# A hybrid streaming encoder on one core: the recurrence of its RWKV-7 layer, by one pair of heads or by two in step

## The chip, the core and the metric

The kernel runs on one core of one Trainium2 chip. The metric is the device time of one execution in microseconds (us). A profile of one execution gives each engine's instructions: PE (matmuls; PEld are its weight loads), DVE, ACT, POOL, and SP, which here issues the DMAs. A trace row of the kernel always carries L210, the line of the helper that emits every instruction, so that rows are told apart by their tiles and shapes.

## The reference, cut to what matters

Four layers of width 2048 are run on 320 tokens (256 of a new stream, 64 of a running one): differential attention, sparse attention, RWKV-7, differential attention. Each is `x <- x + W_out (mixer(rmsnorm(x)) * silu(gate))`. The change is in the third, whose state update for each of 32 heads of 64 channels is

```
def step(st, inp):
    r_t, w_t, k_t, v_t, kk_t, a_t = inp
    sa = einsum('bhvk,bhk->bhv', st, -kk_t)
    st = st * w_t + sa[..., None] * (kk_t * a_t) + v_t[..., None] * k_t
    return st, einsum('bhvk,bhk->bhv', st, r_t)
...
o = (o - mean) * rsqrt(var + GN_EPS)      # per head
o = (o * ln_w + ln_b + bonus) * silu(g)
```

## The kernel before, in words

**Data.** Everything is kept channel-major: 16 tiles of 128 channels by 320 tokens. Index p (0 to 15) names such a tile, which in the RWKV-7 layer is a pair of heads. A projection is a set of output tiles; each is 16 x 3 products of a 128x128 weight block (split in a high and a low part in `ring`) with a 128x320 operand, in four pieces of four blocks. These are the wide products: psum<-op_b,ring for layers whose operand lies in op_b, psum<-op_a,ring for op_a.

**The recurrence** is computed in chunks of 64 tokens: four chunks of the new stream (c = 0 to 3) and one of the running stream. `chains()` (line 2201) goes over p. For each it runs `load_chain(p)` (1971), which waits for one of four sets of SBUF (SETS, 1953) and loads the record of p by DMA (rec_d, yr_d, two of v_d, the state). Then it spawns `chain(ps)` (2039), a task:
- `corners` (2007): per p a PSUM bank, ten 32x32 products, copies on ACT, ten more products, copies, and two scalings on POOL;
- four steps c, the first with the running stream's chunk beside it. A step is: products with 128 rows into a scratch, a copy on ACT, products with 64 rows, a copy with sign on ACT (`put`, 1990), products with 128 rows, the state update on DVE, and copies of the state to the two heads' places on ACT and DVE, from which the next step reads; POOL scales the state for it (`apart`, 2001);
- the set is handed back, and `gated(p)` (2114) is spawned: copy, mean, square, variance, a power on POOL, multiplication, ten 64x64 transposing products (psum<-cst or psum<-cst,arena), the gate; the PSUM bank is handed back behind that (2147).

In the loops of `corners` and `chain`, `for x in now` runs over all p of the task: each phase is emitted for all of them before the next phase.

**Beside it** PE works on the 16 g tiles of the gate's projection (768 wide products, op_b), and after them on the layer's output projection, whose first group is six output tiles together (`out_groups`, 709 and 763).

**What sets the order.** The program is laid down once, by a list scheduler at build time. The main loop (2352) lays down the wide products one block at a time; before each it calls `Sched.pump` (266), which lays down every task instruction whose inputs are ready by the scheduler's own reckoning (for PE with a slack of 400 ns). Where the main loop lacks something (an operand, weights, an accumulator) it calls `force` (288), which moves that reckoning on until a task gets further; nothing wide is laid down meanwhile. On the chip each engine and each DMA queue then runs its instructions in the order laid down.

**PSUM banks.** Of eight banks two are accumulators, and six (2 to 7) are shared (`Banks`, 347). Each p holds one from its corners to the end of `gated`. `start_group` (2335) takes a bank for every tile of a group before the group's first product, so that the group of six takes both accumulators and four of the six shared banks:

```
for mt in g.mts:
    acc = None if g.kis else banks.take_acc()
    while acc is None:
        if banks.free and (g.outer or len(banks.free) > 3):
            acc = banks.take1()
            break
        sched.force("accumulator")
```

In the trace a recurrence product (32, 64 or 128 rows, 32 or 64 columns) shows as two weight loads and two matmuls, a wide product as one.

Of the kernel before, what the change touches and what calls it, by code (L numbers as in the profile page):

```python
# [17 lines left out]
KT = 16  # L18
# [433 lines left out]
def hybrid_kernel(ctx: ExitStack, tc: tile.TileContext, a, o, layers=DEPTH):  # L452
# [62 lines left out]
    def spawn(stage, gen):  # L515
        assert stage.active or not stage.closed
        stage.active += 1
        sched.do(lambda: sched.tasks.append(Task(stage, wrap(stage, gen))))
# [1050 lines left out]
    def layer_c(li, opo, prev):  # L1569
# [388 lines left out]
        def prep_g():  # L1958
            for c in sets:
                G.memset(fields(c)[6], 0.0)  # L1960
            flags["prep_g"] = True
            yield

        def more_sets():

            while not sl.done():
                yield
            yield from wait(("inv", len(batches) - 1))
            sched.do(lambda: ES.free.extend(late))

        def load_chain(p):
            n = [i for i, ps in enumerate(batches) if p in ps][0]
            yield from wait(("inv", n), "prep_g")
            got = yield from SETS.get()
            cm, cs, y, kt, pc, zf, zb = fields(got.ap)
            Q.dma_start(got.ap[:, 0:REC], rec_d[p])
            Q.dma_start(c5(y, 160), y_rows(p))
            for e in range(2):
                Q.dma_start(cs[HALF[e], 320 - 320 * e:640 - 320 * e], v_d[p, HALF[e]])
                G.memset(cs[HALF[e], 320 * e:320 * e + 64], 0.0)  # L1980
            Q.dma_start(zf[:, 64:128], a["state_c_wkv"][p])
            flags["load", p] = got
# [213 lines left out]
        def start_g():  # L2196
            sk.closed = True
            spawn(sg, prep_g())
            spawn(sg, more_sets())

            def chains():
                for p in range(0, KT, 1):
                    ps = range(p, p + 1)
                    for x in ps:
                        yield from load_chain(x)
                    spawn(sg, chain(ps))
            spawn(sg, chains())
# [144 lines left out]
    for n, p in enumerate(pieces):  # L2352
# [17 lines left out]
        for i, b in [(i, b) for i in range(4) for b in range(len(woven))]:  # L2370
# [3 lines left out]
            ps = mt.acc.ap[0:m, 0:T]  # L2374
# [138 lines left out]
```

## Time and profile before

| | us |
|---|---|
| median of 3 runs | 2683.32 (2681.83 to 2683.38) |
| the profiled execution, its own time | 2683.37 |
| its span, first to last instruction | 2681.6 |
| PE busy in the span | 2627.8 (98%) |
| DVE, ACT, POOL busy | 1884.1, 1447.9, 421.4 |
| first product of the recurrence on PE | at 1700.90 |
| last product of the recurrence on PE | at 1903.06 |

Times in rows count from the start of the span. The stretch from 1700.90 to 1903.8 is the one in which the recurrence runs beside the g tiles. A window row gives the busy time of each engine and PE's granted clock (1.00 is full speed); a timeline row gives start, duration, engine, operation, tiles, shape, number of merged instructions and, in brackets, the engine's idle time ahead of it with what ended it.

### The profile page before, as it was taken

The page shows a single profiled execution, that of the slowest core. Times are in us where ns is not written, and L with a number is a line of the kernel's source. Part 1 is how long each engine was busy: PE and PEld are TensorE (multiplying, and loading weights), DVE is VectorE, ACT ScalarE, POOL GpSimd, SP SyncE. Part 2 cuts the span into 40 slices and gives each one's busy share as a digit, 9 for nine tenths or more (in the row PEclk, how much of TensorE's full clock was granted, in tenths as well). Part 3 has the DMA queues.
Part 4 walks back from the last instruction along what each step waited for, and adds up shares of the span by engine and source line. Part 5 has one row for each costly group of instructions (what it writes and reads, how often), then busy time and mean ns, then how long its engine had stood idle before and what let it go on. Part 6 is the DMA issues. An engine that isn't in the chain of part 4 may idle for free.

```text
span 2681.6 us, 53719 instructions
## 1 busy us (share of the span) xinstructions
PE 2627.8 (98%) x20012; PEld 2560.8 (95%) x20012; DVE 1884.1 (70%) x4035; ACT 1447.9 (54%) x3477; POOL 421.4 (16%) x787
## 2 busy tenths in 40 slices
PE   9999999999999999999999999999999999999997
PEld 9999999999999999999999988888999999999997
DVE  7777777665899766459876768457657777777654
ACT  5655555554444544535654544577545655555553
POOL 2000000001000000112011725587310000000011
PEclk9999999999999999999999999999999999999999
DMA  7544444455434334555667777766564444444353
GB/s 233 170 148 159 151 150 151 154 174 184 139 138 147 126 132 147 183 171 172 221 182 200 219 190 205 252 231 196 175 199 159 151 152 152 152 152 152 138 178 107
DMA packets 220876, 455.26 MB, mean 170 GB/s; under 512 B 83398, under 2 KB 149382, under 8 KB 186950
## 3 DMA queue, kind: packets, MB, share of 16 engines
q1 hardware_dynamic: 220614, 451.83, 51.0%
q8 instruction: 157, 2.57, 0.4%
q14 instruction: 105, 0.86, 0.1%
HBM read 394.20 MB, written 57.55 MB: 168 GB/s over the span
## 4 chain that ended last, share of the span: by engine, by line
PE 81%; DVE 6%; ACT 6%; DMA 4%; issue 2%; POOL 1%; SPq 1%; DVEq 0%; POOLq 0%; ACTq 0%
PE psum L210 81%; ACT arena L210 4%; DVE arena L210 4%; DVE ring L210 1%; DMA rec_d<-arena 1%; ACT ring L210 1%; SPq L210 1%; DMA raw<-in_a_w_in_dram 0%; DMA raw<-in_c_w_rkvg_dram 0%; POOL arena L210 0%; DMA arena<-yr_d 0%; DMA bv_d<-arena 0%; DVE op_b L210 0%; ACT op_b L210 0%; DMA yr_d<-arena 0%
## 5 line engine op out<-in xcount | busy, mean ns | idle before, releaser
L210 PE MATMUL psum<-op_a,ring 128*128 128x320 f32 x8496 | 1316.6, 312 | 8.8 <-ACT op_a L210 3.8
L210 PEld LDWEIGHTS psum<-op_a,ring 128*128 128x128 f32 x8496 | 1257.4, 189 | 14.9 <-ACT op_a L210 4.4
L210 ACT CAST ring<-raw 128x512 fp32r<-128x512 f32 (+2 forms) x1228 | 750.0, 618 | 772.7 <-PE psum L210 716.4
L210 DVE TENSOR_TENSOR ring<-raw,ring 128x512 fp32r<-128x512 f32 (+2 forms) x1228 | 855.1, 703 | 402.6 <-ACT ring L210 387.9
L210 PE MATMUL psum<-op_b,ring 128*128 128x320 f32 (+1 forms) x6240 | 990.0, 314 | 0.4 <-DVE arena L210 0.4
L210 PEld LDWEIGHTS psum<-op_b,ring 128*128 128x128 f32 (+1 forms) x6240 | 923.9, 188 | 10.9 <-DVE arena L210 0.7
L210 DVE TENSOR_TENSOR arena<-psum,arena 32x320 f32<-32x320 f32 (+1 forms) x535 | 260.6, 487 | 71.4 <-PE psum L210 61.7
L210 PE MATMUL psum<-arena 128*64 128x64 f32 (+7 forms) x3556 | 267.9, 248 | 8.8 <-DMA arena<-yr_d 3.3
L210 PEld LDWEIGHTS psum<-arena 128*64 128x64 f32 (+5 forms) x3556 | 224.9, 153 | 42.4 <-issue 13.0
L210 ACT ACTIVATE arena<-psum,smt 64x128 f32<-64x128 f32 (+5 forms) x384 | 157.8, 412 | 70.7 <-PE psum L210 49.7
L210 ACT COPY arena<-psum 128x384 f32<-128x384 f32 (+7 forms) x348 | 137.3, 401 | 102.4 <-PE psum L210 97.4
L210 POOL TENSOR_TENSOR arena<-arena 128x64 f32<-128x64 f32 (+25 forms) x282 | 175.7, 631 | 69.0 <-DVE arena L210 40.8
L210 POOL TENSOR_TENSOR smt<-smt,mhalf 128x3 f32<-128x3 f32 (+2 forms) x64 | 68.8, 1075 | 496.6 <-DVE smt L210 496.2
L210 PE MATMUL psum<-cst,arena 128*128 128x128 f32 (+3 forms) x899 | 124.9, 269 | 15.2 <-DVE arena L210 6.8
L210 PEld LDWEIGHTS psum<-cst,arena 128*128 128x128 f32 (+3 forms) x899 | 97.1, 138 | 27.5 <-DVE arena L210 10.1
L210 POOL MEMSET smt<- 128x3 f32 x64 | 6.4, 99 | 680.6 <-DVE smt L210 680.5
L210 POOL TENSOR_TENSOR ssum<-ssum,arena 128x320 f32<-128x320 f32 x70 | 65.3, 933 | 282.2 <-ACT arena L210 281.5
L210 ACT ACTIVATE arena<-arena 128x320 f32<-128x320 f32 (+1 forms) x208 | 90.4, 442 | 34.9 <-DVE arena L210 23.5
L210 ACT CAST op_b<-arena 128x320 fp32r<-128x320 f32 (+4 forms) x198 | 79.4, 417 | 52.4 <-DVE arena L210 32.8
L210 DVE TENSOR_TENSOR op_b<-arena,op_b 128x320 fp32r<-128x320 f32 (+4 forms) x198 | 87.7, 460 | 7.2 <-ACT op_b L210 7.1
L210 DVE TENSOR_TENSOR arena<-arena 64x320 f32<-64x320 f32 (+5 forms) x196 | 85.7, 449 | 2.1 <-ACT arena L210 0.3
L210 ACT CAST op_a<-arena 128x320 fp32r<-128x320 f32 (+2 forms) x127 | 55.8, 441 | 58.0 <-DVE arena L210 39.2
(115 smaller groups left out, 1330.7 us busy)
## 6 DMA issues: line engine op xcount, KB each, us to landing
raw<-in_a_w_in_dram SPq DMA_DIRECT2D x120, 1024.0 KB, 4.9
raw<-in_c_w_rkvg_dram SPq DMA_DIRECT2D x52, 1024.0 KB, 5.3
raw<-in_w_out_dram SPq DMA_DIRECT2D x46, 1024.0 KB, 5.2
raw<-in_b_w_in_dram SPq DMA_DIRECT2D x45, 1024.0 KB, 4.8
raw<-in_w_out_dram SPq DMA_DIRECT2D x72, 256.0 KB, 3.7
arena<-rec_d SPq DMA_DIRECT2D x16, 962.5 KB, 7.7
raw<-in_c_w_rkvg_dram SPq DMA_DIRECT2D x48, 256.0 KB, 3.9
out_dram<-arena SPq DMA_DIRECT2D x72, 160.0 KB, 4.6
```

Source lines behind the costliest of these rows:

```text
L210: return getattr(self.engines[op.eng], op.name)(*op.args, **op.kw)
```

## The change

`chains()` goes over p in steps of two and gives both to one `chain` task. Both loads stand ahead of that task. With four sets, two such tasks of two can be under way; before, four tasks of one.

```
             def chains():
-                for p in range(0, KT, 1):
-                    ps = range(p, p + 1)
+                for p in range(0, KT, 2):
+                    ps = range(p, p + 2)
                     for x in ps:
                         yield from load_chain(x)
                     spawn(sg, chain(ps))
```

No instruction is added or removed; the build lays them down in another order from the recurrence's first products on. In the rows below, 128x320 is a wide product, arena 32x32 a corner, arena 64x64 a product of a step (of 64 or 128 rows), cst 64x64 and cst,arena 64x64 a transposing product of `gated`.

On PE, where the recurrence begins (p = 0 and 1, beside the first g tiles), one piece of the difference:

```order
-L210 MATMUL psum<-op_b,ring 128x320 x9
-L210 MATMUL psum<-arena 32x32 x10
-L210 MATMUL psum<-op_b,ring 128x320 x12
-L210 MATMUL psum<-arena 64x64 x4
+L210 MATMUL psum<-op_b,ring 128x320 x30
+L210 MATMUL psum<-arena 32x32 x10
+L210 MATMUL psum<-op_b,ring 128x320 x3
+L210 MATMUL psum<-arena 32x32 x10
```

Products of the recurrence now come in blocks of two head pairs with fewer returns to the wide ones. From the first corner product to the last wide product of the output projection, the wide products stood in 106 blocks and now stand in 83; the recurrence's products, counted by their number of rows (32, 64 or 128), stood in 184 uniform blocks and now in 126.

On PE, where the g tiles end and the output projection (op_a) begins, before:

```order
L210 MATMUL psum<-cst,arena 64x64 x10
L210 MATMUL psum<-arena 64x64 x6
L210 MATMUL psum<-op_b,ring 128x320 x15
L210 MATMUL psum<-arena 64x64 x2
L210 MATMUL psum<-op_b,ring 128x320 x6
L210 MATMUL psum<-arena 64x64 x8
L210 MATMUL psum<-cst,arena 64x64 x10
L210 MATMUL psum<-op_a,ring 128x320 x45
L210 MATMUL psum<-cst 64x64 x10
L210 MATMUL psum<-op_a,ring 128x320 x723
```

and with the change, directly behind the last block of g products (three of them):

```order
L210 MATMUL psum<-arena 64x64 x56
L210 MATMUL psum<-cst 64x64 x10
L210 MATMUL psum<-cst,arena 64x64 x20
L210 MATMUL psum<-arena 32x32 x30
L210 MATMUL psum<-cst 64x64 x10
L210 MATMUL psum<-arena 32x32 x10
L210 MATMUL psum<-arena 64x64 x96
L210 MATMUL psum<-cst,arena 64x64 x10
L210 MATMUL psum<-arena 32x32 x10
L210 MATMUL psum<-cst,arena 64x64 x10
L210 MATMUL psum<-arena 32x32 x20
L210 MATMUL psum<-op_a,ring 128x320 x6
```

Before, only the last products of p = 15 stood behind the g tiles. Now 282 products of the recurrence stand in a row there: the second half of the last step of p = 8 and 9, the last two steps of 10 and 11, the whole of 12 and 13, and most of the corners of 14 and 15, whose steps stand among the first 162 wide products of the output projection.

On DVE in the same place, the mean of p = 10 (second row), its variance (fifth) and its multiplication (last), with the change:

```order
L210 SCALAR_TENSOR_TENSOR rstd<-psum,cvec,rstd 128x320
L210 SCALAR_TENSOR_TENSOR arena<-smt,arena 128x320
L210 SCALAR_TENSOR_TENSOR rstd<-rstd,cvec,cst 128x320
L210 SCALAR_TENSOR_TENSOR arena<-psum,cvec,arena 128x320
L210 TENSOR_REDUCE smt<-psum 128x5
L210 SCALAR_TENSOR_TENSOR arena<-arena,cvec 128x320
L210 TENSOR_TENSOR op_a<-rstd,op_a 128x320
L210 TENSOR_SCALAR smt<-smt 128x5
L210 TENSOR_TENSOR op_a<-arena,op_a 128x320
L210 TENSOR_REDUCE smt<-cst 128x5
L210 SCALAR_TENSOR_TENSOR cst<-smt,cst 128x320
L210 TENSOR_TENSOR arena<-arena,smt 128x320
```

The rows between belong to `gated` of p = 8 and 9 (the gate, rows with cvec and op_a) and of p = 11 (rows with cst), which end one group and lie on one engine together.

## Rows read from the trace of the kernel before

**Rows 1.** The page: busy time of PE, and its granted clock in 40 slices.
```profile
PE 2627.8 (98%) x20012; PEld 2560.8 (95%) x20012; DVE 1884.1 (70%) x4035; ACT 1447.9 (54%) x3477; POOL 421.4 (16%) x787
...
PEclk9999999999999999999999999999999999999999
```

**Rows 2.** Waits of PEld, 1700.5 to 1904: us in total, times, longest.
```profile
PEld psum L210 <- issue: 10.6, 54, 0.3
PEld psum L210 <- ACT arena L210: 10.6, 44, 0.8
```

**Rows 3.** Timeline of PEld in the recurrence.
```profile
1708.98 0.44 PEld L210 LDWEIGHTS psum<-op_b,ring 128*128 128x128 f32 x3
1709.61 0.31 PEld L210 LDWEIGHTS psum<-arena 64*64 64x64 f32 x8 [0.19 <-issue]
1709.99 0.45 PEld L210 LDWEIGHTS psum<-op_b,ring 128*128 128x128 f32 x3
...
1829.63 0.19 PEld L210 LDWEIGHTS psum<-arena 64*64 64x64 f32 x4 [0.19 <-ACT arena L210]
1829.89 0.45 PEld L210 LDWEIGHTS psum<-op_b,ring 128*128 128x128 f32 x3
...
1896.27 6.60 PEld L210 LDWEIGHTS psum<-op_a,ring 128*128 128x128 f32 x45
```

**Rows 4.** Timeline, ACT and DVE, one step of p = 15.
```profile
1891.38 0.28 DVE L210 SCALAR_TENSOR_TENSOR arena<-psum,arena 128x64 f32<-128x64 f32 x1
...
1891.69 0.24 ACT L210 COPY arena<-arena 64x64 f32<-64x64 f32 x1 [1.15 <-DVE arena L210]
...
1893.16 0.21 ACT L210 COPY arena<-psum 128x64 f32<-128x64 f32 x1 [0.34 <-PE psum L210]
```

**Rows 5.** Timeline of p = 15: corners, last step, last products, its multiplication in `gated`.
```profile
1867.13 0.39 PEld L210 LDWEIGHTS psum<-arena 32*32 32x32 f32 x20 [0.19 <-issue]
...
1892.75 0.20 PEld L210 LDWEIGHTS psum<-arena 128*64 128x64 f32 x4 [0.19 <-issue]
...
1895.04 0.43 PEld L210 LDWEIGHTS psum<-arena 128*64 128x64 f32 x12 [0.76 <-ACT arena L210]
...
1901.71 0.49 DVE L210 TENSOR_TENSOR cst<-cst,smt 128x320 f32<-128x320 f32 x1 [0.42 <-POOL smt L210]
```

**Rows 6.** Groups by form, 1690 to 1900: count | busy us, mean ns | idle ahead.
```profile
L210 ACT ACTIVATE arena<-psum 64x64 f32<-64x64 f32 x160 | 34.8, 217 | 12.6 <-PE psum L210 10.4
...
L210 ACT COPY arena<-arena 64x64 f32<-64x64 f32 x80 | 19.5, 243 | 13.7 <-DVE arena L210 11.5 <-DMA arena<-in_state_c_wkv_dram 1.1
L210 POOL TENSOR_TENSOR smt<-smt,mhalf 128x5 f32<-128x5 f32 x15 | 18.5, 1236 | 3.3 <-DVE smt L210 3.0
...
L210 ACT COPY arena<-psum 128x64 f32<-128x64 f32 x64 | 13.3, 213 | 11.1 <-PE psum L210 9.9
...
L210 ACT ACTIVATE arena<-psum 32x160 f32<-32x160 f32 x32 | 9.4, 293 | 1.0 <-PE psum L210 0.6
...
L210 DVE TENSOR_REDUCE smt<-psum 128x5 f32<-128x320 f32 x16 | 7.7, 482 | 4.1 <-ACT psum L210 4.1
...
L210 ACT ACTIVATE arena<-psum 128x320 f32<-128x320 f32 x14 | 6.1, 436 | 2.7 <-POOL arena L210 1.6 <-PE psum L210 0.8
```

**Rows 7.** Windows: length, busy time (count) of PE, PEld, DVE, ACT, POOL, PEclk, DMA.
```profile
1699.60:1706.30 6.70, 5.39 (x54) 4.94 (x55) 1.18 (x2) 2.85 (x9) 4.31 (x10) 0.50 1.09 331
1706.40:1895.00 188.60, 186.09 (x2928) 153.90 (x2927) 121.83 (x298) 136.05 (x503) 143.15 (x300) 1.00 0.64 207
```

**Rows 8.** Timeline of PEld where the recurrence begins.
```profile
1700.90 0.61 PEld L210 LDWEIGHTS psum<-arena 32*32 32x32 f32 x20 [3.56 <-DMA arena<-yr_d]
1701.58 2.37 PEld L210 LDWEIGHTS psum<-op_b,ring 128*128 128x128 f32 x9
```

**Rows 9.** Timeline of SP: the record of p = 15 is asked for.
```profile
1858.26 0.37 SPq L210 DMA_DIRECT2D arena<-rec_d  x1
```

**Rows 10.** The page's DMA issues: out<-in, count, KB each, us to landing.
```profile
arena<-rec_d SPq DMA_DIRECT2D x16, 962.5 KB, 7.7
```

## The prediction

> **What bounds the kernel now.** I read the page first: PE is busy for 98% of the span and its clock is full in every slice [rows 1]. So only two things can change the time: what PE spends on its own products, and stretches in which PE has nothing to do. Then the waits of the weight loads while the recurrence runs [rows 2]: 98 waits of 0.19 to 0.8 us, about 21 us together. Most of them are no wait for data: the timeline shows the same 0.19 wherever a block of wide products ends and a product of the recurrence begins [rows 3]. That is the first thing to see: today's recurrence is hidden almost completely, and what it costs beside its products is the change of kind. The second is how long the recurrence takes by itself: p = 15 goes from its corners at 1867.13 to its last products at 1895.04, 27.9 us for 20 corner products and 48 others [rows 5]. It is latency; it is hidden as long as wide products lie between its steps.
>
> **The change, term by term.** Nothing is added, so the sum is made of order alone.
>
> *Changes of kind, a gain.* In a run of 45 wide products one weight load follows another after (6.60 - 0.19) / 44 = 0.146 us. A block of three starts at 1708.98 and the next kind at 1709.61: 0.63, of which 3 x 0.146 = 0.44 is work, so 0.19 to 0.20 is the change. Eight loads of a recurrence product need 0.38 (1709.61 to 1709.99), four need 0.26 (1829.63 to 1829.89): 0.03 a load, and 0.14 for the change [rows 3]. The new order has 83 blocks of wide products for 106, and 126 uniform blocks of the recurrence for 184. 23 x 0.20 + 58 x 0.14 = 12.7 us saved.
>
> *A bare stretch, a loss.* The order has 282 recurrence products in a row behind the last g product. A group of two hands its two sets back together, so the next group's loads start late, and in the end the 768 g products are used up while four head pairs are still to come. The output projection cannot fill in: its first group needs four of the six shared banks, and two groups hold four until `gated` is through. Only behind p = 13's transposing products does a wide product come. Now each link has its full length. A step alone, from rows 4 to 6: product to ACT 1893.16 - 1892.75 = 0.41, copy 0.21, ACT to PE about 0.05, second product to ACT 0.41, two copies with sign 2 x 0.217, 0.05, third product to DVE 0.41, state update 0.28, DVE to ACT 0.03, copy 0.24, 0.05: 2.6 us [rows 4, 5, 6]. The second head pair of the group runs inside these gaps; I take 2.65 for both. The stretch is then:
> - the last two steps of p = 10 and 11, 5.3, with 8's and 9's last half step and `gated` on the same in-order ACT and DVE (some seven passes of about 0.44, 3.1; the group at 436 ns is the row for such a pass [rows 6]): 8.5;
> - `gated` of p = 10, whose bank p = 13 needs: from the last products at 1895.04 to the end of the multiplication at 1902.20 it took 7.2 [rows 5]; now six closing rows of 8 and 9 stand between its own on DVE, so I take no less: 7.2;
> - corners and first step of p = 12 and 13. ACT carries eight copies of 0.29, four of the state at 0.24, then two of 0.21, four at 0.22, eight more at 0.22, two of 0.24: 6.8, and three links of 0.41 [rows 4, 6]: 8.0;
> - three more steps: 8.0;
> - `gated` of 12 and 13: 7.2, and one POOL power of 1.24 more for the second [rows 5, 6]: 8.4.
>
> That is 40.1 us; I take 40. PE's own work in it is 212 x 2 x 0.03 + 70 x 2 x 0.016 (0.39 for 20 loads [rows 5]) + 23 x 0.14 = 18, done before as well. So PE waits 22 us. Bounds: with `gated` at the length of its parts (power 1.24, two sums at 0.48, five passes of about 0.45: 4.5 [rows 6]) and without the 3.1 of the others, 32; with 27.9 + 7.2 for p = 12 and 13 as p = 15 took it, and the first two items, 51 [rows 5]. The wait is 14 to 33. The value lies nearer the low end because p = 15's 27.9 has wide products in it that are gone here.
>
> *The clock.* Before the first corners PE waited 3.56 us [rows 8], and the granted clock then was 0.50 for 6.7 us [rows 7]: nine wide products took 2.37, (2.37 - 0.19) / 8 = 0.27 each for 0.146. The bare stretch has several waits of that size, so the clock should stand at its lower level, 1.2 GHz, where the projection begins: 6.7 us at 0.27 are 25 products, 3 us lost. Bounds 0 (the clock holds) and 6 (it is also low inside the stretch, where each of some 25 links with products grows by about 0.1). I take 3.
> The Trainium skill ("TensorE: Matmul & The Clock Gate", on the clock gate) says that an idle PE falls back to half its rate until it has been busy again. By that rule the term is at its upper end, 6; the trace agrees as far as the one episode in rows 7 goes.
>
> *Loads.* The loads of both stand ahead of a group's task, in the same SP queue as the weights, with the state's load behind the store of the old state. Before, p = 15's record was asked for at 1858.26 and its corners ran at 1867.13, 8.9 us later, with no wait [rows 5, 9]; the order keeps wide products for about such a time, but now two records come at once, for p = 4 to 11 twice. The price of a missed one is the first one's, 3.56 [rows 8]; between 0 and 4 x 3.56 I take 1.5, since none of the reloads was missed before.
>
> *After it* the steps of p = 14 and 15 have 162 wide products between them, three and more at each link, and `gated` behind them 45, as p = 15 had; I cost them at nothing. From the end of the output projection on PE's order is the same, so the rest shifts as a whole.
>
> Sum: -12.7 + 22 + 3 + 1.5 = +13.8 us on the profiled execution's 2683.37 (the median is 2683.32, no different): **2697**.
>
> **The rivals.**
> 1. *The stretch is shorter than thought and the saved changes win* (faster). For it: the 12.7 is the firmest term, from rows that repeat to 0.01 us, while the 40 is put together by hand. It decides where the bare stretch is under 18 + 12.7 = 30.7 us with the clock at full speed: at 25 us, 2683.4 - 12.7 + 7 = 2677.7, and 2670.7 if it costs nothing. Against it: 30.7 is under the low bound of 32.
> The Trainium skill ("TensorEngine Tiling (Array Packing)", Key Properties) says that changing the tiling mode drains TensorE; by this rule alone the change gains its 12.7 us and nothing more. The 0.14 and 0.20 of rows 3 agree with it.
> 2. *They cancel* (no change): a stretch of 28 to 35 us, the low bound with little loss of clock: 2681 to 2688.
> 3. *The reloads are late* (slower still): four times 3.56 in the middle of the stage, on top of the sum instead of 1.5: 2697 + 12.7 = 2710. For it: two records of 962.5 KB [rows 10] and their companions are asked for at once. Against it: no such wait before.
>
> **How the numbers follow.** About 0.2%, 5.4 us, is what a measurement of this kernel can tell from no change. I give the forecast 0.62, rival 1 0.10, rival 2 0.16, rival 3 0.12. Slower by more than that: 0.62 + 0.12 = 0.74; within it 0.16; faster 0.10. With the bounds of the wait alone the forecast runs from 2689 to 2708. The range reaches down over rival 2 and up over rival 3 with some of its spread: 2681 to 2713.
>
> **What would show it.** Right: wide products until about 1855, then some 40 us with PE's loads busy for less than half, the first op_a product at about 1894, the last transposing product at about 1934 (before, 1903, with 117 fewer wide products done); waits of PEld for ACT and DVE arena tiles of several us; a stretch at 0.50 in the granted clock there; ahead of it, the waits of 0.19 fewer by about a fifth or more. Wrong: a stretch under 31 us; the loss spread over the stage with DMA as releaser (rival 3); or a loss outside 1700 to 1935, for which this argument has no place.

## The result and the profile after

The changed kernel takes 2707.42 us (median of 4 runs, 2705.45 to 2709.12) where the kernel before took 2682.57 beside it: a ratio of 1.0088, 95% interval 1.0076 to 1.0100, 24.9 us slower. The forecast was 2697 in a range of 2681 to 2713. The profiled execution took 2709.12 us; its span is 2707.3.

The page of the changed kernel, busy time and granted clock, to be read against [rows 1]:

```profile
PE 2637.2 (97%) x20012; PEld 2571.9 (95%) x20012; DVE 1885.9 (70%) x4035; ACT 1453.7 (54%) x3477; POOL 425.1 (16%) x787
...
PEclk9999999999999999999999999997899999999999
```

The same number of products keeps PE busy 9.4 us longer, and two slices have lost clock, where before none had. Windows of the changed kernel tell where; the columns are those of [rows 7]:

```profile
1703.50:1857.20 153.70, 151.49 (x2217) 131.86 (x2217) 90.81 (x208) 105.48 (x372) 113.62 (x229) 0.98 0.66 213
1857.20:1908.00 50.80, 34.08 (x565) 28.20 (x564) 27.32 (x72) 24.70 (x93) 25.94 (x56) 0.59 0.47 148
1908.00:1946.60 38.60, 38.60 (x420) 34.30 (x414) 18.99 (x45) 20.25 (x65) 13.30 (x28) 0.92 0.30 95
```

The second window is the bare stretch: 282 recurrence products (564 loads), 28.2 us of loads in 50.8. Its ends and its inside in the timeline of PEld:

```profile
1856.62 0.45 PEld L210 LDWEIGHTS psum<-op_b,ring 128*128 128x128 f32 x3
1857.25 0.69 PEld L210 LDWEIGHTS psum<-arena 64*64 64x64 f32 x16 [0.19 <-ACT arena L210]
...
1865.09 1.36 PEld L210 LDWEIGHTS psum<-arena 128*64 128x64 f32 x24 [0.42 <-ACT arena L210]
...
1873.68 1.18 PEld L210 LDWEIGHTS psum<-cst,arena 64*64 64x64 f32 x20 [4.90 <-ACT psum L210]
...
1887.48 0.54 PEld L210 LDWEIGHTS psum<-arena 128*64 128x64 f32 x8 [1.18 <-ACT arena L210]
...
1891.05 0.30 PEld L210 LDWEIGHTS psum<-arena 128*64 128x64 f32 x4 [0.31 <-ACT arena L210]
...
1903.81 1.17 PEld L210 LDWEIGHTS psum<-cst,arena 64*64 64x64 f32 x20 [5.44 <-issue]
...
1908.06 1.57 PEld L210 LDWEIGHTS psum<-op_a,ring 128*128 128x128 f32 x6
1909.95 0.61 PEld L210 LDWEIGHTS psum<-arena 32*32 32x32 f32 x20 [0.33 <-issue]
1910.63 2.37 PEld L210 LDWEIGHTS psum<-op_a,ring 128*128 128x128 f32 x9
...
1945.91 0.66 PEld L210 LDWEIGHTS psum<-cst,arena 64*64 64x64 f32 x20 [0.19 <-issue]
```

The last g products start at 1856.62, the first op_a at 1908.06, the last transposing products at 1945.91. The first rows of the waits of PEld from 1700.5 to 1942 (us in total, times, longest), against [rows 2]:

```profile
PEld psum L210 <- ACT arena L210: 18.3, 59, 1.5
PEld psum L210 <- issue: 13.1, 40, 5.4
PEld psum L210 <- ACT psum L210: 4.9, 1, 4.9
PEld psum L210 <- DMA arena<-yr_d: 3.7, 1, 3.7
```

The one wait for a load is that of the very first corners, as before [rows 8]: no reload is late. Ahead of the stage, where the order of PE is the same in both kernels, the profiled execution had lost 2.6 us already (first corners at 1703.49, 1700.90 before [rows 8]); from the end of the stage on the two traces run parallel, 25.7 us apart. So some 23 of the 25.8 us between the two profiled executions arise between 1703 and 1946.

### The profile page after: what moved, and what is told of

The parts are those of the page before. It is cut to its first block, busy times and chain, and to the rows that moved or that the text cites. A ratio compares the mean times of both kernels' runs of the same rounds, so it can differ in the third digit from the quotient of the medians.

```text
span 2707.3 us, 53766 instructions
## 1 busy us (share of the span) xinstructions
PE 2637.2 (97%) x20012; PEld 2571.9 (95%) x20012; DVE 1885.9 (70%) x4035; ACT 1453.7 (54%) x3477; POOL 425.1 (16%) x787
## 4 chain that ended last, share of the span: by engine, by line
PE 79%; ACT 7%; DVE 6%; DMA 4%; issue 2%; POOL 1%; SPq 0%; DVEq 0%; POOLq 0%; ACTq 0%
PE psum L210 79%; ACT arena L210 6%; DVE arena L210 4%; DVE ring L210 1%; ACT ring L210 1%; DMA arena<-yr_d 1%; POOL arena L210 1%; DMA arena<-l_d 1%; DVE smt L210 1%; DMA raw<-in_a_w_in_dram 0%; DMA bv_d<-arena 0%; SPq L210 0%; ACT op_a L210 0%; DMA yr_d<-arena 0%; DMA arena<-in_x_dram 0%
## 5 line engine op out<-in xcount | busy, mean ns | idle before, releaser
L210 PEld LDWEIGHTS psum<-arena 128*64 128x64 f32 (+5 forms) x3556 | 229.7, 160 | 47.6 <-ACT arena L210 18.5
L210 ACT COPY arena<-psum 128x320 f32<-128x320 f32 (+8 forms) x350 | 137.1, 403 | 105.2 <-PE psum L210 99.3
L210 POOL TENSOR_TENSOR arena<-arena 128x64 f32<-128x64 f32 (+24 forms) x282 | 177.3, 633 | 74.1 <-DVE arena L210 45.1
L210 ACT CAST op_b<-arena 128x320 fp32r<-128x320 f32 (+4 forms) x198 | 79.7, 418 | 50.8 <-DVE arena L210 32.1
```

The lines of the kernel that those rows point to most:

```text
L210: return getattr(self.engines[op.eng], op.name)(*op.args, **op.kw)
```

## The experiments

There were twelve runs of ten new kernels, one of them twice, and of the changed kernel once more; the kernel before ran beside each. Their traces reach the first corner at different times (1699.6 to 1708.2), though the order of PE ahead of it is the same, so that stages are compared by their length. "Bare" products are recurrence products without a wide one between them, in the order laid down.

### A smaller first group, and its control

The first group of the output projection takes four tiles, so that it needs two shared banks and not four; the control does the same to the kernel before.

```
-        return ([Group(mts[0:(6 if li == 2 else 4)], ...
+        return ([Group(mts[0:(4 if li == 2 else 4)], ...
```

> The changed kernel, with one edit: the output projection's first group in this layer takes four output tiles instead of six, so two shared banks instead of four, and it can begin while two groups of head pairs still hold theirs. In the order laid down the first output-projection product now follows the g tiles at once; the longest runs of recurrence products without a wide one are 92, 70 and 38 instead of 282. Theory A (the bare stretch behind the g tiles is the loss: 50.8 us for about 18 us of PE's own work, and it exists because of the banks): about 33 us come back, and some 3 us of half clock behind it, so 2671; with up to 9 us of waits left in the three shorter runs, 2671 to 2680, below the kernel before by 3 to 12 us, which is the saving of changes of kind (91 wide blocks for 106, 126 uniform ones for 184). Rival B (pairs in step lose time all over the stage, by later loads or longer links, and the stretch is only where it becomes visible): the time stays over 2690. Rival C (the stretch is the loss, but the changes of kind are hidden anyway): 2682 to 2686, no faster than before.

> Control for the run with a first group of four: the kernel before with the same edit. Its group of six never waited for banks, so all theories expect the time of before within 3 us, 2680 to 2686. If it were faster by itself by 5 us or more, the group size would be a gain of its own and the other run would have to be read against this one.

The control: 2685.39 us, ratio 0.9997 (0.9988 to 1.0006). The changed kernel with it: 2701.43 us against 2685.28, ratio 1.0046 (1.0032 to 1.0060). Less than half of the loss has gone: theory A's size is wrong, and by the total alone rival B (over 2690) stands; the next section decides against it. The five times spread over 12.8 us (2692.59 to 2705.43) and the trace is that of the slowest. Its windows and timeline of PEld:

```profile
1860.80:1888.60 27.80, 27.78 (x406) 23.98 (x404) 19.64 (x47) 18.93 (x65) 15.54 (x34) 1.00 0.82 266
1888.60:1937.30 48.70, 37.11 (x604) 30.43 (x600) 27.71 (x71) 25.77 (x100) 24.80 (x52) 0.83 0.32 106
```

```profile
1914.51 1.39 PEld L210 LDWEIGHTS psum<-arena 128*64 128x64 f32 x40 [0.19 <-issue]
...
1929.57 0.19 PEld L210 LDWEIGHTS psum<-op_a,ring 128*128 128x128 f32 x1 [2.04 <-ACT op_a L210]
1930.80 1.12 PEld L210 LDWEIGHTS psum<-op_a,ring 128*128 128x128 f32 x5 [1.04 <-DVE op_a L210]
```

Where 50.8 us were bare, PE is now full for 28 us, and then it starves all the same. By 1914.51 it has done 144 op_a products, which is three quarters of the 4 x 48 of the group; by the order of the group the next ones need op_a of p = 12; they come at 1929.57, and they wait for op_a, from ACT and then from DVE. The banks were the gate that I had seen; behind it stands a second one, the operands, and a smaller group reaches it sooner.

### Cover that is not missing

If the rest of the argument holds, the change must pay where wide work is plentiful. Both kernels got 300 more wide products at the start of that group, with the scheduler's tasks between them:

```
             mt.acc = acc
+            if mt is g.mts[0] and len(g.mts) == 6 and not g.weave:
+                for i in range(3 * 100):
+                    if i % 3 == 0:
+                        sched.pump()
+                    model.emit(Op("PE", "matmul", (acc.ap[:, 0:T],), dict(lhsT=blk, rhs=op_b[:, 0, 0, :], ...
```

> The kernel before with 300 wide products more between the g tiles and the output projection (into an accumulator that is then overwritten; results unused), so that the recurrence has cover beyond its end. All theories: 2683 plus 300 x 0.146 = 43.8 us, 2725 to 2730; 108 wide blocks and 184 uniform ones in the order laid down. It is the control for the next run.

> The changed kernel with the same 300 wide products. No bare stretch is left in the order laid down (longest run without a wide product 42); 99 wide blocks for 108 of the control, 129 uniform ones for 184. Theory A (changes of kind cost 0.20 and 0.14 us, and all the rest of the loss is the missing cover): 9 x 0.20 + 55 x 0.14 = 9.5 us below the control, 2716 to 2720, clock 1.00. Rival N (the changes of kind cost nothing, or pairs in step bring new waits for loads, ACT or DVE even under cover): the control's time or more, 2725 to 2735.

Without the change 2725.45 us (2723.68 to 2728.62), with it 2719.19 (2717.29 to 2720.89): 6.3 us faster, two thirds of the 9.5; no time of one lies among the other's. Waits of PEld from 1699 to 1932, the kernel before first:

```profile
PEld psum L210 <- issue: 10.8, 56, 0.3
PEld psum L210 <- ACT arena L210: 9.8, 43, 0.6
```

```profile
PEld psum L210 <- ACT arena L210: 10.0, 43, 0.7
PEld psum L210 <- issue: 9.4, 49, 0.2
PEld psum L210 <- DMA arena<-yr_d: 4.7, 3, 3.7
```

Pairs in step bring almost no new wait while they are covered: 4.7 us for loads where the kernel before has 3.6. So the saving is real, and the loss of the change is missing cover; rivals B and N fall.

### PE kept busy in the bare stretch

```
                 sched.force("accumulator")
+                while g.outer and sched.tasks and model.clk["PE"] + 600.0 < sched.now:
+                    model.emit(Op("PE", "matmul", (g.mts[0].acc.ap[:, 0:T],),
+                                  dict(lhsT=blk, rhs=op_b[:, 0, 0, :], start=True, stop=True)))
```

> The changed kernel, with PE kept busy in the bare stretch: where the first group of the output projection lacks a bank and PE would run dry, a wide product into an accumulator that is already taken is added (98 of them, whose results are overwritten and used by nothing). They add 98 x 0.146 = 14.3 us of PE work into a stretch in which PE waits for 33. Theory A1 (ten of the eleven us by which the stretch is longer than my 40 come from PE running it at half clock): granted clock 1.00 throughout, stretch of 40 to 43 us, total 2693 to 2699. Rival L (the stretch is long because the links on ACT, DVE and POOL are long, whatever PE's clock): clock 1.00, but the stretch stays at 48 to 52 us, total 2703 to 2710. If the added products come in the way of the links, longer still.

> The kernel with 98 wide products added in the bare stretch once more, on another day's chip, because its first times spread over 10 us. From the first corner product to the layer's end its trace took 8 us less than the changed kernel's. If that is PE's clock, it comes again: granted clock 1.00, the stretch 44 to 46 us instead of 50 to 51, and a ratio to the kernel before of 1.004 to 1.007 where the changed kernel has 1.0076 and 1.0088. If the stretch is back at 50, it was chance.

> The changed kernel itself once more, on the chip of the three runs beside it, so that they can be read against it: 2705 to 2711, with the bare stretch of 49 to 52 us at half clock from 1857 on.

With the added products: 2705.39 us against 2685.28, ratio 1.0070 (1.0057 to 1.0083), and again, on another chip, 2699.83 against 2683.26, ratio 1.0063 (1.0050 to 1.0076). The changed kernel once more: 2708.03 against 2687.10, ratio 1.0076 (1.0061 to 1.0090). The mean of the ratios, 1.0067 for 1.0082, is 4 us in favour of the added work; the intervals overlap, so that the total alone says little, and the first total lies in rival L's range, not in A1's. The traces say more. From the first corner to the end of the span they take 996.1 and 997.2 us with the added products, 1003.8 and 1005.1 in the changed kernel. The stretch with the added products, twice, and in the repeated changed kernel:

```profile
1857.50:1903.00 45.50, 38.51 (x665) 32.47 (x663) 26.09 (x72) 23.78 (x93) 26.04 (x56) 1.00 0.53 165
```

```profile
1853.00:1900.80 47.80, 39.87 (x665) 33.80 (x663) 26.09 (x72) 23.90 (x94) 26.08 (x56) 0.96 0.51 157
```

```profile
1862.40:1912.70 50.30, 33.38 (x566) 27.50 (x564) 27.55 (x72) 24.67 (x94) 25.62 (x56) 0.62 0.49 149
```

The stretch is 2.5 to 5.3 us shorter, though 14 us of work are added. The clock is full in the first and nearly so in the second, where one block of nine wide products took 2.37 us for 1.32. Neither theory has it right: A1 said 40 to 43 us, L 48 to 52, and the repeat missed its 44 to 46. One step of p = 12 and 13, first with the added products (PEld, then DVE), then in the changed kernel (DVE; its PEld row of 1891.05 stands above):

```profile
1888.35 0.31 PEld L210 LDWEIGHTS psum<-arena 128*64 128x64 f32 x8 [0.19 <-issue]
...
1890.94 1.32 PEld L210 LDWEIGHTS psum<-op_b,blk 128*128 128x128 f32 x9
1892.46 0.31 PEld L210 LDWEIGHTS psum<-arena 128*64 128x64 f32 x8 [0.19 <-issue]
```

```profile
1890.68 0.28 DVE L210 SCALAR_TENSOR_TENSOR arena<-psum,arena 128x64 f32<-128x64 f32 x1 [2.95 <-PE psum L210]
```

```profile
1890.44 0.28 DVE L210 SCALAR_TENSOR_TENSOR arena<-psum,arena 128x64 f32<-128x64 f32 x1 [2.88 <-PE psum L210]
...
1894.25 0.28 DVE L210 SCALAR_TENSOR_TENSOR arena<-psum,arena 128x64 f32<-128x64 f32 x1 [2.66 <-PE psum L210]
...
1898.09 0.28 DVE L210 SCALAR_TENSOR_TENSOR arena<-psum,arena 128x64 f32<-128x64 f32 x1 [2.69 <-PE psum L210]
```

From the first product of the step to the state update it takes 1890.68 - 1888.35 = 2.33 us at full clock, and 1894.25 - 1891.05 = 3.20 at half. The half clock costs 0.87 us a step. The state copies follow within another 0.6, so a step at full clock would be 2.9 us long by the first head pair (an estimate; by the second, whose copies end 0.5 later, 3.4), where the changed kernel has 1894.25 - 1890.44 = 3.81. The added work itself takes some of the gain back: nine products, 1.32 us together, lie between the steps and make each one 1892.46 - 1888.35 = 4.11 long.

### What makes the g tiles run out early

> The changed kernel with half of the change undone: both loads still stand ahead of a pair of head pairs, but each head pair is a task of its own again, not in step. The order laid down is nearly that of before (115 wide blocks, 201 uniform ones; longest bare run 48). Theory A (what uses up the g tiles early is that two head pairs in step hand their sets and banks back together): no bare stretch; 2683 plus 9 x 0.20 + 17 x 0.14 = 4.2 us for more changes of kind, 2684 to 2690. Rival J (the joint load, which starts the second head pair's record late or early, is what costs): 2697 or more, with waits for loads or a bare stretch.

```
-                    spawn(sg, chain(ps))
+                    for x in ps:
+                        spawn(sg, chain([x]))
```

> The changed kernel with each head pair a task of its own, not in step, but the two sets of a group still loaded together and handed back together, when both head pairs are through. The prediction said that the joint hand-back is why the next loads start late and the g tiles run out (theory H). Theory E: it is the emission in step, in which each head pair's link waits for the other's copies on ACT, that makes a set's turn longer (64 us for the first turn where single head pairs took 47). H: the turn of the sets stays near 60 us and the time at 2700 or more. E: turns of 47 to 53 us, and 2683 plus 13 x 0.20 + 12 x 0.14 = 4.3 us for more changes of kind, 2684 to 2691, with no bare stretch (119 wide blocks, longest bare run 50).

```
-                got.rel()
+                flags["fin", p] = True
...
+        def back(ps):
+            yield from wait(*[("fin", p) for p in ps])
+            for p in ps:
+                flags["load", p].rel()
...
+                    spawn(sg, back(ps))
```

(The chains are single, as in the run before.) Loaded together but not in step: 2687.73 us, ratio 1.0011 (1.0002 to 1.0019). Handed back together as well: 2689.26 against 2686.61, ratio 1.0014 (1.0005 to 1.0023). Theory H falls, and so does rival J. The pace is read from SP's timeline, the loads of p = 0, 4 and 12: that of p = 4 waits for a set to come round once, that of p = 12 three times. Before:

```profile
1690.27 0.32 SPq L210 DMA_DIRECT2D arena<-rec_d  x1
...
1737.19 0.37 SPq L210 DMA_DIRECT2D arena<-rec_d  x1
...
1833.04 0.39 SPq L210 DMA_DIRECT2D arena<-rec_d  x1
```

The changed kernel:

```profile
1692.74 0.32 SPq L210 DMA_DIRECT2D arena<-rec_d  x1
...
1756.71 0.38 SPq L210 DMA_DIRECT2D arena<-rec_d  x1
...
1859.69 0.37 SPq L210 DMA_DIRECT2D arena<-rec_d  x1
```

Joint hand-back without step:

```profile
1691.28 0.32 SPq L210 DMA_DIRECT2D arena<-rec_d  x1
...
1742.74 0.37 SPq L210 DMA_DIRECT2D arena<-rec_d  x1
...
1842.64 1.37 SPq L210 DMA_DIRECT2D arena<-rec_d  x1
```

The first turn of a set takes 46.9 us before, 64.0 with the change, 51.5 with the joint hand-back alone; three turns take 142.8, 167.0 and 151.4. Loaded together alone, the same loads stand 46.1 and 143.9 us apart. So a third of the 24 us that the recurrence falls behind is the joint load and hand-back, nearly all of it the hand-back, and two thirds are the step itself. One piece of it shows in the first group, in the changed kernel's PEld and DVE and in the DVE of before:

```profile
1703.49 0.61 PEld L210 LDWEIGHTS psum<-arena 32*32 32x32 f32 x20 [3.71 <-DMA arena<-yr_d]
...
1710.93 0.39 PEld L210 LDWEIGHTS psum<-arena 32*32 32x32 f32 x20 [0.19 <-issue]
```

```profile
1723.00 0.28 DVE L210 TENSOR_SCALAR arena<-psum,arena 128x64 f32<-128x64 f32 x1 [4.46 <-ACT arena L210]
```

```profile
1712.61 0.28 DVE L210 TENSOR_SCALAR arena<-psum,arena 128x64 f32<-128x64 f32 x1 [3.41 <-PE psum L210]
```

p = 0 has its corners begun at 1703.49, but in step it stands until p = 1 has begun its own at 1710.93: its first state update comes 19.5 us after its first corner, before 11.7. PE is busy all the while with g products: nothing is lost there, it is only taken from the end.

### The pace alone, and half the pairs

> The kernel before with three sets of SBUF for single head pairs instead of four; no head pairs in step anywhere. Theory P (the loss comes from the pace of the recurrence: a set came round every 47 to 49 us before, every 64, 54 and 49 us with the change, so the g tiles run out too early, and the rest of the recurrence is bare): three places at 47 us give the same kind of loss without any pairing. In the order laid down 322 recurrence products stand bare behind the g tiles; at the change's excess of (50.8 - 18) / 282 = 0.116 us each that is 37 us, plus 3 of clock and 2.4 of more changes of kind (200 uniform blocks for 184): 2727, between 2712 and 2740. Rival S (what costs is the emission in step itself: both head pairs on the in-order ACT and DVE, double bursts): less than 2700, since nothing is in step.

```
-        sets = [lg.ap(SET) for _ in range(4)]
+        sets = [lg.ap(SET) for _ in range(3)]
```

> The changed kernel with single head pairs for p = 0 to 7 and pairs in step for p = 8 to 15. In the order laid down 216 recurrence products stand bare. Theory P: 216 x 0.116 = 25 us, plus 3 of clock, less 5.5 for 12 and 22 fewer changes of kind: 2707, between 2698 and 2714. Rival S (cost in proportion to the pairs in step): half of the loss of 25: 2695 to 2698. The two lie close, the next run parts them.

```
-                for p in range(0, KT, 2):
-                    ps = range(p, p + 2)
+                for p in [*range(0, 8), *range(8, KT, 2)]:
+                    ps = range(p, p + (1 if p < 8 else 2))
```

> The reverse: pairs in step for p = 0 to 7, single head pairs for p = 8 to 15. In the order laid down 350 recurrence products stand bare, although nothing is in step in that stretch. Theory P: 350 x 0.116 = 41 us, plus 3 of clock, less 11.2 for 31 and 36 fewer changes of kind: 2718, between 2706 and 2726, slower than with all pairs in step. Rival S: half of the loss, 2695 to 2698.

```
+                for p in [*range(0, 8, 2), *range(8, KT)]:
+                    ps = range(p, p + (2 if p < 8 else 1))
```

All beside 2687.10 us of the kernel before. Three sets: 2711.24, ratio 1.0089 (1.0075 to 1.0103). Single first, pairs last: 2702.24, ratio 1.0057 (1.0045 to 1.0070). Pairs first, single last: 2693.81, ratio 1.0027 (1.0017 to 1.0037). Rival S falls with the first, where nothing is in step and the loss is the change's own. Theory P has the size in the second alone; where single head pairs stand bare it is 16 and 24 us too high, outside its range both times, and in the last run S's figure is the nearer, though the measured time is below S's range too. The windows of the bare stretch, of the three runs in this order:

```profile
1871.40:1918.20 46.80, 37.17 (x646) 30.71 (x645) 24.64 (x67) 28.64 (x114) 25.65 (x63) 0.62 0.41 126
```

```profile
1875.40:1910.20 34.80, 23.62 (x433) 20.44 (x432) 17.23 (x50) 18.42 (x75) 19.22 (x41) 0.67 0.31 90
```

```profile
1865.70:1910.30 44.60, 35.49 (x702) 29.76 (x700) 26.37 (x74) 29.09 (x120) 29.72 (x67) 0.73 0.55 164
```

A bare product costs 50.8 / 282 = 0.180 us and 34.8 / 216 = 0.161 where two head pairs in step stand there, 46.8 / 322 = 0.145 and 44.6 / 350 = 0.127 where single chains do; PE is busy for 37.2 and 35.5 us there instead of 34.1. That single chains fill each other's gaps is the likely reason; no run tests it. The clock is higher in the last alone (0.73; the change has 0.59 and 0.62). With the prediction's 18 / 282 = 0.064 of PE's own work for each product, and its prices for the changes of kind, the sum can be made for all four:

| kernel | bare stretch | own work | changes of kind | sum | measured |
|---|---|---|---|---|---|
| the change | 50.8 | 18.0 | -12.7 | +20.1 | +24.9, +20.9 |
| three sets | 46.8 | 20.6 | +2.4 | +28.6 | +24.1 |
| single, then pairs | 34.8 | 13.8 | -5.5 | +15.5 | +15.1 |
| pairs, then single | 44.6 | 22.4 | -11.2 | +11.0 | +6.7 |

Made afterwards, with the measured stretch, the sum is within 5 us each time. No kernel that was run beats the kernel before.

## Why the prediction was right, and where it was off

**What bounds the kernel:** right. PE is full until 1857, nothing outside the stage has moved for a reason that the change gives, and the changed sum is made of order alone.

**Changes of kind, -12.7:** the sign is right, the size somewhat high. With full cover 6.3 us came back of 9.5 worked out by the same prices. The waits fell as said, from 43 + 37 to 31 + 34 before 1857, about a fifth; but that sign proves little, because by then PE had done 1680 loads other than those of the g tiles, where it had done 1958 before, a seventh fewer. For each load the waits are 5% fewer.

**The bare stretch, 40 us:** this term is the mis-sized one. Its place and its start are right (wide products until 1857, said 1855), and so are the banks, as the first of two gates: the smaller group showed the operands behind them. But it lasts 50.8 us, to 1908 and not to 1894. Item by item, from the timeline above: 7.8 for 8.5, 8.6 for 7.2, 13.8 for 8.0 (corners and first step), 10.9 for 8.0 (three steps, to the end of p = 12's last state update at 1898.4), 9.7 for 8.4. More than half of the 10.8 us too many lies in the corners and first step, 2.9 in the three steps. The step of 2.65 us was a little short at full clock (2.9 to 3.4, as worked out above); at half clock it is 3.8, and some 42 of the 50.8 us ran so. What of the corners' 5.8 is the clock alone, no run separates. Two of the signs named beforehand did not come: PE's loads were busy for 28.2 of 50.8 us, more than half, and the waits for ACT arena tiles were 1.5 us at most (the two long waits, 4.9 and 5.4, have other releasers).

**The clock, 3 us with an upper end of 6:** this is where it failed. I let the clock fall in the waits and cost it behind the stretch. Windows inside the changed kernel's stretch, PEclk being the third number from the end:

```profile
1857.20:1862.60 5.40, 3.95 (x77) 3.03 (x76) 3.98 (x13) 4.57 (x18) 3.55 (x13) 1.00 0.39 99
1862.70:1869.40 6.70, 5.67 (x77) 4.74 (x76) 4.29 (x12) 2.08 (x9) 4.60 (x10) 0.50 1.04 351
1869.50:1872.80 3.30, 0.00 (x0) 0.00 (x0) 3.22 (x9) 1.45 (x4) 2.14 (x2) 1.00 1.13 347
1872.90:1913.80 40.90, 30.16 (x455) 25.44 (x457) 17.62 (x45) 20.01 (x73) 18.08 (x40) 0.50 0.28 88
```

It stood at 0.50 twice, for 47.6 us together, the second time from inside the wait of 4.90 us to 1913.8, although PE's loads were busy for 25.4 of these 40.9 us. And its price lies in the links, 0.87 us for the three of a step, where I had "about 0.1" a link as the upper end. PE's loads take 28.2 us in the stretch; with the added products they take 32.5, of which 14.5 are the added ones, so 18.0 at full clock. If all of the 10.2 between lies in the chain, the stretch at full clock would be 50.8 - 10.2 = 40.6 us, about the forecast (an estimate; by the filled kernel's 45.5 less three times 4.11 - 2.93 it is 42). So the clock cost some 9 to 10 us in the stretch and not behind it. Behind it, 15 op_a products at 0.27 for 0.146 cost 1.9.
The Trainium skill ("TensorE: Matmul & The Clock Gate", "A second HAM failure mode") says that brief idle gaps between groups of matmuls can make the clock swing between its levels. The trace agrees in part: the clock fell at 1862.6 after waits of at most 0.63 us, was back at 1.00 from 1869.4 to 1872.9 while PE had nothing to run, and fell again; but then it stayed down for 40.9 us.

**Why the cover ends early:** the prediction put it down to two sets handed back together. Loaded and handed back together they are a third of it; the step itself is two thirds.

**Loads, 1.5 us, and rival 3:** nothing; no reload was waited for. **After the stretch** no wait is left among p = 14 and 15, as said; the last transposing products come at 1945.9 for 1934, of which the stretch's excess is 10.8.

So the forecast's own sum with the wait and the clock as found is -12.7 + 32.8 + 1.9 = +22.0 us for the 23 between the profiled executions in the stage. The -12.7 was not measured in this kernel; at two thirds of it, as with full cover, the sum is +26. The direction was safe, since rival 1 needed a stretch under 30.7 us. That 2707 lies within the bounds of the forecast is in part luck: it was 13.8 us for 24.9, its upper bound of 51 us came from p = 15's time with wide products in it and not from the clock, and the range reached on to 2713 for late reloads, which did not come.

## What to carry to other kernels

Work that is hidden has a pace, and when the cover is of fixed length a slower pace does not show where it arises but at the end of the cover: compare the times at which a resource comes round (here the loads of a set) before counting what is saved on the bounding engine. Doing two dependency chains in step saves changes of kind on PE, but in step one head pair waits for the other (seen here in the first group); with ample cover that paid here (6.3 us), without it independent chains were better. Where PE is left with short dependent products, price its links at the lower clock, not at the clock of the profile before.

## What the runs showed of the hardware that was not expected

The granted clock was 1.00 for 3.3 us in which PE did nothing (1869.5 to 1872.8), and then 0.50 for 40.9 us in which PE's loads were busy for 25.4, in pieces of 0.3 to 2.4 us. Added products of no use, which took 14 us, made the same stretch shorter by 2.5 to 5.3 us.

The program ahead of the recurrence reached the first corner product at times from 1699.6 to 1708.2 us in the fourteen traces. Late ones mostly had more time at 0.50 ahead of it (21.5 us in the earliest, 44.4 in the latest), but it does not go by the clock alone: a trace with 23.9 came at 1704.1, one with 27.3 at 1700.8. Why stays open. A single profiled execution of this kernel can thus be several us off for no cause in the change.
